# Ordering a product-key router's keys by summed exponentials instead of counts

## The chip, the cores and the metric

One core of one Trainium2 chip runs the kernel in one launch. Its engines, by the names of the profile, are PE (matrix products; PEld is its weight load), DVE (vector), ACT (scalar functions), POOL (which also issues the indirect gathers) and SP (which issues most plain transfers). Each works through an instruction list of its own, and they wait for each other on semaphores. The metric is device time of the launch in microseconds (us), lower is better.

## What the reference computes, where the change acts

The layer is an attention mixer on 512 tokens of 1024 features and then a product-key expert layer (PEER). Only the second is touched:

```python
q = (xb @ w_query).reshape(128, 8, 2, 128)               # 8 heads, two half queries
s = jnp.einsum('chpd,hpnd->chpn', q, sub_keys)           # scores against 128 keys per half
top_s, top_i = lax.top_k(s, 16)
cand_s = top_s[:, :, 0, :, None] + top_s[:, :, 1, None, :]
best_s, pos = lax.top_k(cand_s.reshape(128, 8, 256), 16) # 16 experts per token and head
g = jax.nn.softmax(best_s, axis=-1)
act = gelu(einsum('cd,chkd->chk', xb, expert_u[idx]))    # of 128 * 128 experts
out = einsum('chk,chkd->cd', g * act, expert_v[idx])
```

## The kernel before, in words

The experts of a head form a grid of 128 by 128 cells (key a of the first half, key b of the second). The kernel sorts both key lists of a head by popularity, and computes the 512 cells of a staircase in the popular corner (`RECTS`, rectangles of rows a0 to a1 and width w) densely for all 512 tokens, in four chunks of 128 experts per head. What a token chose outside the staircase is gathered: the tokens are sorted by how many such pairs they have, and each of the four sorted blocks of 128 tokens gets a fixed number of gathered columns (`TAIL`); what tokens have beyond goes to 128 further rows of `FOLD` = 4 pairs each. One column is one expert row (u and v, 8 KB) per token: a POOL gather of the expert's number (`tid`), a POOL gather of the row (`tuv`), a DVE product with the token's row that gives the dot product (`tscr`, L1903), and a DVE multiply-add to the token's sum (`tacc`, L1825). If 128 rows don't hold what is left, a loop (`tail_rest`) takes the remainder.

Time falls into three stages: the mixer (to about 350 us), the routing of the eight heads (to about 600 us), and the stage in which gathered columns are mixed with the rest of the dense experts (to about 1000 us), with a short end.

The routing runs in periods, one call of `route` per period i. A period mixes steps of four heads: L = head i (best 16 of both lists, pairs, best pairs), N = head i + 1 (second query, ranking of its keys, scores), M = head i + 2 (weights, first query), and B = head i - 1 (count, softmax weights, the dense cells' weights `dexp`). `dn(0)` to `dn(3)` put a quarter of a dense chunk each in between. Inside `in_order` every engine executes its instructions in the order in which the Python code emits them, so an instruction that waits holds back all that stands behind it on its engine. `best_pairs`, the last step of a period on DVE, yields the bound `tb` (L1357); ACT's count (`cm`, L1375) of the next period waits for it.

The ranking of N's keys (`rank1` to `rank3`, L1209 to L1255): PE computes the scores of the first block's 128 tokens (`pss`), DVE marks each token's best eight (`m8s`, `ind`), PE counts the marks of each key in two layouts (`psc`), DVE subtracts a tie-breaker (`pkey`), counts for each key how many keys are greater (`pjunk`, `prank`) and builds a permutation matrix (`pm`); `rank3` lets PE permute the keys (`psk`), ACT copies them (`kp`), and DVE forms the table of expert numbers (`tabs`, L1250), which SP stores.

Of the kernel before, what the change touches and what calls it, by code (L numbers as in the profile page):

```python
# [17 lines left out]
T = 512  # L18
D = 1024
NB = 4  # L20
# [10 lines left out]
# Cells (a, b) of a head's key grid, in popularity order, whose experts are computed for all tokens.  # L31
RECTS = ((0, 2, 60), (2, 6, 31), (6, 14, 20), (14, 32, 6))
CELLS = sum((a1 - a0) * w for a0, a1, w in RECTS)
NCH = CELLS // 128
# Gathered pairs per token, for the four blocks of tokens sorted by their number. What tokens have beyond goes to 128
# more rows of FOLD pairs each, as many to a token as it needs. When those don't do, a loop takes the rest instead.
TAIL = (29, 21, 16, 11)
# [18 lines left out]
# What the steps of dense and gathered experts take of the tensor engine, of the memory's bandwidth and of the vector  # L56
# engine, relative to each other.
# [9 lines left out]
# Ranks (a, b) of the two key lists that can be among the 16 best sums: (a + 1) * (b + 1) <= 16.  # L67
# [96 lines left out]
def build(tc, A, out):  # L164
    nc = tc.nc
    with ExitStack() as ctx:
# [9 lines left out]
        # The two parts of the rows that the large products take: the mixer's input, its outcome, the experts' input.  # L176
# [12 lines left out]
def rsq_steps(nc, y, t, v):  # L189
    """y = 1 / sqrt(v) to float32's accuracy."""  # L190
    nc.vector.tensor_scalar(t.bitcast(I32), v.bitcast(I32), 1, None, op0=OP.arith_shift_right)
    nc.vector.tensor_scalar(y.bitcast(I32), t.bitcast(I32), -1, 0x5F3759DF, op0=OP.mult, op1=OP.add)
    for _ in range(3):
        yield
        nc.vector.scalar_tensor_tensor(t, y, -0.5, y, op0=OP.mult, op1=OP.mult)
        nc.vector.tensor_tensor(t, t, v, op=OP.mult)
        yield
        nc.vector.scalar_tensor_tensor(y, t, 1.5, y, op0=OP.add, op1=OP.mult)


def rsq(nc, pool, v, n):
    """1 / sqrt(v) of a [128, n] tile."""
# [7 lines left out]
def rsq1(nc, pool, ss, n):  # L210
    """1 / sqrt(mean + EPS) of n values, from two sums of squares, in steps; h: minus half the mean."""
# [19 lines left out]
def sum_sq(nc, G, pool, ss, x, first, last, bufs=2):  # L231
    """Adds the squares of a tile [features, T] to the tokens' sums, [128, NB] of a bank."""
# [21 lines left out]
def row_bcast_of(nc, G, cols, pool, PS, tag, ptag=None):  # L254
    """Columns [128, n] as a row of 128 n tokens on all partitions; returns what does the product, to PSUM."""
# [18 lines left out]
def norm_shift(nc, hH, hL, z, sh):  # L274
    """The modulated rows in two parts."""
# [6 lines left out]
def load_split(tc, pool, src, tag, eng, raw=2, bufs=2, rpool=None):  # L282
    """A weight tile as float32r parts: high bits, and what they leave."""
# [7 lines left out]
def split(nc, pool, w, tag, eng, bufs=2):  # L291
    """High bits, and what they leave."""
# [16 lines left out]
def ada(tc, A, G, pool, m, ca, w):  # L309
    """Sums of a modulation's products over each partition's rows, in steps; loads run one ahead. For all but the first,  # L310
    scalar and GpSimd engines share the work, as the vector engine has other work then."""
# [31 lines left out]
def ada_start(tc, A, G, P1, AD, PS, m, ca, bcol):  # L343
    """A modulation whose products the tensor engine shares, as it has nothing else to do at the start; in steps."""
# [55 lines left out]
def ada_rest(tc, A, G, P1, PS, ca, bcol):  # L400
    """The modulations that the start doesn't need, in 43 steps."""
# [83 lines left out]
class Outward:  # L485
    """The outward projection by halves of the tokens: x1, and its rows for the experts."""
# [10 lines left out]
    def prepare(self, n):  # L497
        """The two parts of the weights' tiles up to n, one step per tile; loads run one ahead. They lie where the
        modulations' weights and the first head group's queries and keys were."""
# [36 lines left out]
    def after(self, half, i):  # L536
        """A tile's squares and its rows of tokens."""
# [21 lines left out]
    def finish(self, half):  # L559
        """A half's normed rows; in steps."""  # L560
# [23 lines left out]
def start(tc, A, G, P1, AD, PW, PS, S, xT, ca, bcol):  # L584
    """The first two modulations; the normed input, scaled, is in km."""
# [3 lines left out]
    # Rows of zeros: the scores' products span the whole array.  # L589
# [34 lines left out]
def project(tc, A, G, W, P1, PW, PS, S, lgain, band, rest, ahead):  # L624
    """The inward projections; what follows a tile's products comes after the next tile's."""
# [52 lines left out]
    def parts(dst, low, src, r):  # L678
        """High bits to some rows, and what they leave to others."""
# [3 lines left out]
    def rotate(i):  # L683
        """Rotary positions, and the parts that the scores' products take."""
# [84 lines left out]
def attention(tc, A, G, P1, PW, more, ups, PS, S, sink, nsink, band, mH, mL, rest, X, out):  # L769
    """Heads in three stages that run a few heads apart: scores, transposes, values. The first heads run beside the  # L770
    last of the projections (ups), whose memory is the attention's after that (more)."""
# [61 lines left out]
    def after(B):  # L833
        """What makes the normed rows of a block of tokens; in steps, the first of which follows the first group."""
# [87 lines left out]
def peer(tc, A, G, DR, out, xpool):  # L922
    nc = tc.nc
    with ExitStack() as ctx:
# [17 lines left out]
        with ExitStack() as c2:  # L942
            # The queries' weights lie where the attention was, so that they are there before the mixer's end.
# [18 lines left out]
            def step(amount):  # L962
                """Dense experts' steps where the routing leaves the tensor engine to them."""
# [26 lines left out]
def start_query(H):  # L990
    """The first head's queries, by halves of the tokens, and the second head's weights."""
# [14 lines left out]
def start_routing(tc, G, H):  # L1006
    """The first head's keys, and the experts' input as rows of tokens for the gathers."""
    nc = tc.nc
    with tc.tile_pool(name="h2p", bufs=1, side="right") as W:
# [9 lines left out]

        H[0].rank1()  # L1020
        rows(0)
        H[0].rank2()
        rows(1)
# [9 lines left out]
def end_routing(tc, A, G, B, WQ, step):  # L1033
    """The last head's weights, and the tokens' order."""
# [34 lines left out]
def first_columns(tc, G, WQ, step):  # L1069
    """The codes of the first gathered columns, and where their experts' rows are."""  # L1070
# [17 lines left out]
def in_order(tc):  # L1088
    """Keeps each engine's instructions in the order they are written in."""
# [1037 lines left out]
```

## Time and profile before

| | |
|---|---|
| median of 3 timed runs | 1040.32 us (1039.12 to 1043.28) |
| span of the profiled execution | 1042.5 us |
| PE, DVE, POOL, ACT busy over the span | 89%, 77%, 54%, 42% |
| mean granted TensorE clock | 0.955 of full speed |
| gathered columns | 81 |

The profiled execution is one of its own. Its span, from the first instruction to the last, is 1042.5 us, 2.2 us over the median of the timed runs and inside their range; what lies around a span is not listed, so the span is read as that execution's time.

### The profile page before, as it was taken

The page shows a single profiled execution, that of the slowest core. Times are in us where ns is not written, and L with a number is a line of the kernel's source. Part 1 is how long each engine was busy: PE and PEld are TensorE (multiplying, and loading weights), DVE is VectorE, ACT ScalarE, POOL GpSimd, SP SyncE. Part 2 cuts the span into 40 slices and gives each one's busy share as a digit, 9 for nine tenths or more (in the row PEclk, how much of TensorE's full clock was granted, in tenths as well). Part 3 has the DMA queues.
Part 4 walks back from the last instruction along what each step waited for, and adds up shares of the span by engine and source line. Part 5 has one row for each costly group of instructions (what it writes and reads, how often), then busy time and mean ns, then how long its engine had stood idle before and what let it go on. Part 6 is the DMA issues. An engine that isn't in the chain of part 4 may idle for free.

```text
span 1042.5 us, 13550 instructions
## 1 busy us (share of the span) xinstructions
PE 928.5 (89%) x4190; PEld 646.5 (62%) x4190; DVE 806.8 (77%) x2284; ACT 439.4 (42%) x937; POOL 565.7 (54%) x569
## 2 busy tenths in 40 slices
PE   7898989999999987898867889899999999999992
PEld 2475648788799776676654457365565747475640
DVE  4628756875555579999999768998668897887987
ACT  2334366555523436677765443042231414142312
POOL 1145711323432268777766375688657767577513
PEclk9999999996899999999988989999999999999997
DMA  8564132421221335453322476986959978788642
GB/s 325 205 229 163 61 114 83 168 86 58 85 76 41 134 115 163 123 156 109 105 68 78 126 292 248 343 324 211 325 212 370 395 255 319 293 326 284 231 168 83
DMA packets 77047, 196.86 MB, mean 189 GB/s; under 512 B 23271, under 2 KB 41063, under 8 KB 64871
## 3 DMA queue, kind: packets, MB, share of 16 engines
q0 software_dynamic: 26400, 118.93, 31.5%
q1 hardware_dynamic: 49848, 76.40, 21.8%
q8 instruction: 33, 0.54, 0.2%
q10 hardware_dynamic: 720, 0.62, 0.2%
q14 instruction: 46, 0.37, 0.1%
HBM read 187.95 MB, written 18.96 MB: 198 GB/s over the span
## 4 chain that ended last, share of the span: by engine, by line
PE 34%; DVE 34%; DMA 7%; issue 6%; POOL 3%; ACT 3%; SPq 0%; DVEq 0%; POOLq 0%; ACTq 0%
PE vacc L1604 9%; DMA tuv<-in_UV,tid 6%; PE udot L1553 5%; PE outp L305 4%; PE ops L831 4%; DVE dexp L1423 2%; DVE tacc L1825 2%; PE sc L807 2%; PE pt L815 2%; DVE tscr L1903 2%; PE q L1201 2%; DVE ti L1295 1%; DVE ti L1299 1%; DVE s L1293 1%; DVE cc L1327 1%
## 5 line engine op out<-in xcount | busy, mean ns | idle before, releaser
L1604 PE MATMUL vacc<-dv,gT 128*128 128x512 f32 x512 | 226.3, 599 | 5.4 <-DVE accd L1578 4.3
L1604 PEld LDWEIGHTS vacc<-dv,gT 128*128 128x128 f32 x512 | 97.7, 192 | 126.2 <-issue 112.5
L1903 DVE SCALAR_TENSOR_TENSOR tscr<-tuv,thp 128x1024 bf16<-128x1024 f32 x81 | 98.8, 1219 | 35.2 <-DMA tuv<-in_UV,tid 35.1
L1825 DVE SCALAR_TENSOR_TENSOR tacc<-tuv,twg,tacc 128x1024 f32<-128x1024 f32 x81 | 103.8, 1281 | 16.1 <-ACT twg L1824 15.9
L156 POOL DMA_INDIRECT tid<-tab,tci x81 | 94.6, 1168 | 29.4 <-issue 23.0
L1553 PE MATMUL udot<-hH,uh 128*128 128x512 f32 x256 | 108.5, 424 | 0.0
L156 POOL DMA_INDIRECT tuv<-in_UV,tid x81 | 93.6, 1155 | 27.0 <-issue 15.8
L1553 PE MATMUL udot<-hH,ul 128*128 128x512 f32 x256 | 102.8, 402 | 0.0
L1553 PE MATMUL udot<-hL,uh 128*128 128x512 f32 x256 | 102.4, 400 | 0.0
L1823 ACT ACTIVATE twg<-tdots 128x1 f32<-128x1 f32 x81 | 16.4, 202 | 149.1 <-DVE tscr L1903 149.1
L327 POOL TENSOR_TENSOR ada_acc<-ada_acc,ada_w 128x1024 f32<-128x1024 f32 x9 | 21.4, 2383 | 88.1 <-issue 30.7
L809 ACT ACTIVATE psb<-psb,anm 128x512 f32<-128x512 f32 (+2 forms) x64 | 40.9, 640 | 56.6 <-DVE psb L808 35.4
L297 POOL TENSOR_TENSOR wl_in<-wraw_in,wh_in 128x1024 fp32r<-128x1024 f32 x10 | 26.0, 2602 | 69.7 <-ACT wh_in L296 69.6
L1190 POOL TENSOR_TENSOR wl_pq<-wraw_pq,wh_pq 128x1024 fp32r<-128x1024 f32 x16 | 38.0, 2378 | 44.3 <-ACT wh_pq L1189 35.4
L1201 PE MATMUL q<-hH,wh_pq 128*128 128x512 f32 (+1 forms) x144 | 56.6, 395 | 0.1
L1553 PEld LDWEIGHTS udot<-hH,ul 128*128 128x128 f32 x256 | 49.0, 191 | 12.2 <-issue 0.2
L1201 PE MATMUL q<-hH,wl_pq 128*128 128x512 f32 (+1 forms) x144 | 54.9, 382 | 1.8 <-POOL wl_pq L1190 1.8
L1538 ACT CAST uh<-ut 128x512 fp32r<-128x512 f32 x64 | 37.3, 583 | 45.2 <-PE ut L1535 45.2
L1201 PE MATMUL q<-hL,wh_pq 128*128 128x512 f32 (+1 forms) x144 | 55.0, 383 | 0.5 <-DVE hL L580 0.5
L1553 PEld LDWEIGHTS udot<-hL,uh 128*128 128x128 f32 x256 | 49.3, 193 | 9.3 <-issue 0.2
L1553 PEld LDWEIGHTS udot<-hH,uh 128*128 128x128 f32 x256 | 49.2, 192 | 8.5 <-issue 0.2
L1546 ACT CAST ul<-ut 128x512 fp32r<-128x512 f32 x64 | 37.4, 584 | 36.0 <-PE ut L1545 35.7
(409 smaller groups left out, 2379.5 us busy)
## 6 DMA issues: line engine op xcount, KB each, us to landing
ada_w<-in_w_ada SPq DMA_DIRECT2D x22, 1024.0 KB
wraw_pq<-in_w_pq SPq DMA_DIRECT2D x16, 512.0 KB
gts<-gts SPq DMA_DIRECT2D x32, 256.0 KB
gT<-gts SPq DMA_DIRECT2D x32, 256.0 KB
wraw_in<-in_w_in SPq DMA_DIRECT2D x10, 512.0 KB
wraw_out<-in_w_out SPq DMA_DIRECT2D x8, 512.0 KB
x1T<-in_xT SPq DMA_DIRECT2D x4, 512.0 KB
ada_w<-in_w_ada SPq DMA_DIRECT2D x4, 512.0 KB
```

The costliest lines, as they stand in the source:

```text
L156: nc.gpsimd.indirect_dma_start(out=out, out_offset=None, in_=src, in_offset=bass.IndirectOffsetOnAxis(ap=idx, axis=0), **kw)
L305: nc.tensor.matmul(ps, a[:, c], b[:, c], start=n == 0, stop=n == 3 * kc - 1)
L809: nc.scalar.activation(U.p, U.p, AF.Exp, bias=nm, scale=-1.0, accum_out=B.den[:, i:i + 1])
L831: nc.tensor.matmul(B.ops[U.grp][:, U.h], U.pt[:, j], vr, start=j == 0, stop=j == U.nk - 1)
L1190: nc.gpsimd.tensor_tensor(wl, self.raw[p], wh.bitcast(F32), op=OP.subtract)
L1201: nc.tensor.matmul(self.q[p][:, cols], a[:, c], b[:, c, cols], start=c == 0 and i == 0, stop=c == KC - 1 and i == 2)
L1538: nc.scalar.copy(uh, pt)
L1546: nc.scalar.copy(ul, pt)
L1553: nc.tensor.matmul(ps, a, b[:, k], start=k == 0 and i == 0, stop=k == KC - 1 and i == 2)
L1604: nc.tensor.matmul(ps, ws[h, k][:, b * 128:(b + 1) * 128], vs[k][:, sl], start=k == 0, stop=k == NCH - 1)
L1825: nc.vector.scalar_tensor_tensor(acc, uv[:, D:], wg, acc, op0=OP.mult, op1=OP.add)
L1903: nc.vector.scalar_tensor_tensor(B.s, uv[:, 0:D], 1.0, B.hp, op0=OP.mult, op1=OP.mult, accum_out=B.dots[:, c])
```

## The change

The popularity of a key becomes the sum over all 512 tokens of exp(0.085 * score), where it was the number of the first 128 tokens that have the key among their best eight. `rank0(p)` computes a half's scores with the keys on partitions (one product of 128x512) and sums their exponentials with one ACT instruction. `rank1` turns the two sums into an ordering key (the upper bits of the number, minus the tie-breaker), copies it along a row on ACT (`pkeyb`) and lets PE transpose that to a row of all keys on every partition (`psc`). `rank2` compares as before. The staircase has five rectangles for four, still 512 cells. `TAIL` goes from 77 to 71 columns, 75 with the four of `FOLD` for 81. Comments are also dropped, which moves line numbers.

```diff
-RECTS = ((0, 2, 60), (2, 6, 31), (6, 14, 20), (14, 32, 6))
+RECTS = ((0, 2, 51), (2, 6, 28), (6, 14, 17), (14, 26, 8), (26, 48, 3))
+KEYSCALE = 0.085
+KEYBITS = 15
-TAIL = (29, 21, 16, 11)
+TAIL = (28, 20, 14, 9)
...
+    def rank0(self, p):
+        nc, R = self.nc, self.R
+        if p == 0:
+            self.stat = R.tile([128, 2], F32, name="stat", bufs=2)
+        ps = self.G.PS.tile([128, T], F32, name="pst", tag="rank")
+        nc.tensor.matmul(ps, self.keys[:, 0, p], self.q[p], start=True, stop=True)
+        junk = R.tile([128, T], BF16, name="pexp", bufs=1)
+        nc.scalar.activation(junk, ps, AF.Exp, scale=KEYSCALE, accum_out=self.stat[:, p:p + 1])
     def rank1(self):
-        for p in range(2):
-            nc.tensor.matmul(pss[:, p], self.q[p][:, 0:128], self.keys[:, 0, p], start=True, stop=True)
-        for p in range(2):
-            nc.vector.max(m8[:, p], pss[:, p])
-        for p in range(2):
-            nc.vector.tensor_scalar(self.ind[:, p], pss[:, p], m8[:, p, 7:8], None, op0=OP.is_ge)
+        bits = R.tile([128, 2], I32, name="pbits", bufs=1)
+        nc.vector.tensor_scalar(bits, self.stat.bitcast(I32), KEYBITS, None, op0=OP.arith_shift_right)
+        self.key = R.tile([128, 2], F32, name="pkey", bufs=2)
+        nc.vector.tensor_tensor(self.key, bits, G.noff, op=OP.subtract)
+        kb = R.tile([128, 2, 128], F32, name="pkeyb", bufs=1)
+        nc.scalar.copy(kb, self.key[:, :, None].to_broadcast([128, 2, 128]))
+        self.psc = G.PS.tile([128, 2, 128], F32, name="psc", tag="rank")
+        for p in range(2):
+            nc.tensor.transpose(self.psc[:, p], kb[:, p], G.ident)
     def rank2(self):
-        nc.tensor.matmul(psc[:, 0:256], G.onesb, self.ind.rearrange("p a b -> p (a b)"), start=True, stop=True)
-        for p in range(2):
-            nc.tensor.matmul(psc[:, 256 + p:257 + p], self.ind[:, p], G.onesb[:, 0:1], start=True, stop=True)
-        nc.vector.tensor_tensor(key, psc, G.noff, op=OP.subtract)
         for p in range(2):
-            nc.vector.tensor_scalar(junk, key[:, p * 128:(p + 1) * 128], key[:, 256 + p:257 + p], None,
-                                    op0=OP.is_gt, op1=OP.add, accum_out=rank[:, p:p + 1])
+            nc.vector.tensor_scalar(junk, self.psc[:, p], self.key[:, p:p + 1], None, op0=OP.is_gt, op1=OP.add,
+                                    accum_out=rank[:, p:p + 1])
...
 def route(G, H, dn, i):
     on(B, "count", 2)
+    on(N, "rank0", 0)
     on(N, "query", 1, 0, KC)
...
     dn(0)
     on(B, "weights")
-    on(N, "rank1")
+    on(N, "rank0", 1)
     for b in range(NB):
         on(B, "scale", b)
     if N is not None:
         G.gelu()
     on(L, "best", 1, 0)
+    on(N, "rank1")
     on(M, "query", 0, 0, 4)
```

On PE, in the fourth period, the list before has the ranking's two small products between the dense step (`udot`) and M's first query (`q`); the counts (`psc`) come twelve query products later.

```order
L1553 MATMUL udot<-hL,uh 128x512
L1553 MATMUL udot<-hH,ul 128x512
L1215 MATMUL pss<-keys,qsb 128x128 x2
L1201 MATMUL q<-hH,wh_pq 128x512
L1201 MATMUL q<-hL,wh_pq 128x512
```

With the change the second half's score product (`pst`) and, right behind it, the transposes of the copied key (`psc`) stand at that place, ahead of M's query.

```order
L1562 MATMUL udot<-hL,uh 128x512
L1562 MATMUL udot<-hH,ul 128x512
L1217 MATMUL pst<-qsb,keys 128x512
L1232 MATMUL psc<-ident,pkeyb 128x128 x2
L1203 MATMUL q<-hH,wh_pq 128x512
L1203 MATMUL q<-hL,wh_pq 128x512
```

So `psc` has moved from behind twelve query products to ahead of them, and reads `pkeyb`, which ACT writes.

On ACT, the same period before, from B's second count to the copy of the turned dense rows (`uh`): the copy of N's second query (`qsb`), B's exponentials and their scaling (`dexp`), and the dense step's gelu (`act`) with its table load.

```order
L1375 ACTIVATE cm,cn<-cand,tb 128x512 x2
L1205 COPY qsb<-q 128x512
L1416 ACTIVATE dexp<-cand,nmx 128x512 x4
L1546 CAST ul<-ut 128x512
L1419 ACTIVATE dexp<-dexp,rzk 128x512 x4
L1558 ACT_TABLE_LOAD
L1558 ACTIVATE act<-udot 128x512
L1538 CAST uh<-ut 128x512
```

With the change:

```order
L1382 ACTIVATE cm,cn<-cand,tb 128x512 x2
L1219 ACTIVATE pexp,stat<-pst 128x512
L1207 COPY qsb<-q 128x512
L1423 ACTIVATE dexp<-cand,nmx 128x512 x4
L1555 CAST ul<-ut 128x512
L1219 ACTIVATE pexp,stat<-pst 128x512
L1426 ACTIVATE dexp<-dexp,rzk 128x512 x4
L1567 ACT_TABLE_LOAD
L1567 ACTIVATE act<-udot 128x512
L1229 COPY pkeyb<-pkey 128x256
L1547 CAST uh<-ut 128x512
```

Two exponentials (`pexp`) have come in, and the copy `pkeyb` stands behind the scaling, the table load and the gelu. The number of table loads in the whole list stays the same.

## Rows read from the trace of the kernel before

**Rows 1.** Windows, one period: us, then busy us of each engine, clock, DMA share, GB/s.

```profile
core 0: us, PE busy (x) PEld busy (x) DVE busy (x) ACT busy (x) POOL busy (x), PEclk, DMA share, GB/s
444.10:472.40 28.30, 25.77 (x135) 20.65 (x134) 27.67 (x137) 20.19 (x35) 21.41 (x32) 1.00 0.57 166
```

**Rows 2.** Timeline of DVE, that period: start, duration, then the idle time and its releaser.

```profile
443.99 0.15 DVE L1357 TENSOR_TENSOR tb<-tb,mx 128x4 f32<-128x4 f32 x1
...
451.75 0.48 DVE L1217 MAX8 m8s<-pss 128x8 f32<-128x128 f32 x2
...
452.67 0.47 DVE L1291 MAX8 lb<-ssb 128x8 f32<-128x128 f32 x2
...
456.74 0.41 DVE L1228 TENSOR_TENSOR pkey<-psc,noff 128x258 f32<-128x258 f32 x1
457.19 0.35 DVE L1233 TENSOR_SCALAR_CACHE_REDUCE pjunk<-pkey 128x128 bf16<-128x128 f32 x1
...
461.50 0.35 DVE L1250 TENSOR_SCALAR tabs<-psk,c 128x128 int32<-128x128 f32 x1
...
472.24 0.17 DVE L1357 TENSOR_TENSOR tb<-tb,mx 128x4 f32<-128x4 f32 x1
```

**Rows 3.** Timeline of ACT, that period.

```profile
444.18 0.72 ACT L1375 ACTIVATE cm<-cand,tb 128x512 bf16<-128x512 f32 x1 [1.29 <-DVE tb L1357]
445.02 0.72 ACT L1375 ACTIVATE cm<-cand,tb 128x512 bf16<-128x512 f32 x1
...
451.93 2.56 ACT L1419 ACTIVATE dexp<-dexp,rzk 128x512 f32<-128x512 f32 x4 [0.18 <-DVE rzk L1396]
...
455.80 0.60 ACT L1558 ACTIVATE act<-udot 128x512 f32<-128x512 f32 x1
456.29 0.58 ACT L1538 CAST uh<-ut 128x512 fp32r<-128x512 f32 x1
...
459.70 0.37 ACT L1246 COPY kp<-psk 128x256 f32<-128x256 f32 x1 [2.34 <-PE psk L1244]
```

**Rows 4.** Timeline of PE, that period.

```profile
448.87 0.49 PE L1215 MATMUL pss<-keys,qsb 128*128 128x128 f32 x2 [0.61 <-ACT qsb L1205]
449.11 0.48 PE L1201 MATMUL q<-hH,wh_pq 128*128 128x512 f32 x1
...
458.28 0.95 PE L1242 MATMUL psk<-pm,keys 128*128 128x128 f32 x4 [0.27 <-DVE pm L1236]
...
459.20 0.47 PE L1244 MATMUL psk<-pm,prow 128*128 128x128 f32 x2
```

**Rows 5.** Chain that ended last, dense work in the gathering stage.

```profile
816.03 0.44 PE ut L1535 x4
816.46 1.40 PE udot L1553 x6
...
829.91 27.47 PE vacc L1604 x64
```

**Rows 6.** ACT and DVE timelines, the third period and the fifth.

```profile
425.29 2.56 ACT L1419 ACTIVATE dexp<-dexp,rzk 128x512 f32<-128x512 f32 x4 [0.19 <-DVE rzk L1396]
...
434.24 0.35 DVE L1250 TENSOR_SCALAR tabs<-psk,c 128x128 int32<-128x128 f32 x1
...
484.06 0.60 ACT L1558 ACTIVATE act<-udot 128x512 f32<-128x512 f32 x1
...
490.16 0.35 DVE L1250 TENSOR_SCALAR tabs<-psk,c 128x128 int32<-128x128 f32 x1
```

**Rows 7.** Windows around two waits of PE, columns as in Rows 1.

```profile
392.50:396.00 3.50, 0.21 (x2) 0.21 (x2) 3.43 (x23) 3.47 (x9) 3.17 (x3) 1.00 0.89 301
396.00:400.00 4.00, 4.00 (x13) 3.13 (x13) 3.65 (x14) 2.94 (x6) 3.36 (x8) 0.57 0.48 185
...
540.00:546.00 6.00, 4.41 (x20) 4.04 (x19) 5.86 (x16) 1.59 (x5) 5.69 (x8) 0.50 0.22 49
```

**Rows 8.** Windows of the gathering stage, columns as in Rows 1.

```profile
600.00:700.00 100.00, 87.75 (x320) 56.87 (x319) 86.62 (x205) 33.34 (x73) 69.69 (x65) 0.95 0.84 309
700.00:1000.00 300.00, 292.85 (x1034) 179.56 (x1033) 247.69 (x416) 88.69 (x235) 202.44 (x170) 1.00 0.79 287
```

**Rows 9.** The gathered rows' tile: operation, count, ns min/median/max, first and last start.

```profile
L1903 DVE SCALAR_TENSOR_TENSOR tscr<-tuv,thp x81: 1155/1218/1286, 618.2 to 996.7; 128x1024 bf16<-128x1024 f32 x81
L1825 DVE SCALAR_TENSOR_TENSOR tacc<-tuv,twg,tacc x81: 1271/1280/1347, 621.9 to 999.2; 128x1024 f32<-128x1024 f32 x81
```

**Rows 10.** DMA queue: packets, MB, share of 16 engines.

```profile
q0 software_dynamic: 26400, 118.93, 31.5%
```

More of the change, by code (lines that the diff above doesn't have):

```diff
@@ L1018, in rows @@
             nc.sync.dma_start(G.hs[b * 128:(b + 1) * 128, :], t)
+        H[0].rank0(0)
+        rows(0)
+        H[0].rank0(1)
+        rows(1)
         H[0].rank1()
-        rows(0)
         H[0].rank2()
-        rows(1)
         H[0].rank3()
@@ L1154, in route_setup @@
     nc = tc.nc
-    G.onesb = R.tile([128, 128], BF16, name="onesb")
-    nc.vector.memset(G.onesb, 1.0)
     G.irow = R.tile([128, 128], F32, name="irow")
@@ L1160, in route_setup @@
     iota(nc, G.prow, [[0, 128]], cm=1)
-    G.noff = R.tile([128, 258], F32, name="noff")
-    iota(nc, G.noff[:, 0:256].rearrange("p (a b) -> p a b", a=2), [[0, 2], [1, 128]])
-    iota(nc, G.noff[:, 256:258], [[0, 2]], cm=1)
+    G.noff = R.tile([128, 2], F32, name="noff")
+    iota(nc, G.noff, [[0, 2]], cm=1)
     nc.vector.tensor_scalar(G.noff, G.noff, 1.0 / 256, None, op0=OP.mult)
@@ L1206, in query @@
             self.q[p] = qt
-    def rank1(self):
-        nc, R = self.nc, self.R
-        pss = self.G.PS.tile([128, 2, 128], F32, name="pss", tag="rank")
-        m8 = R.tile([128, 2, 8], F32, name="m8s", bufs=2)
-        self.ind = R.tile([128, 2, 128], BF16, name="ind", bufs=1)
-        for p in range(2):
-            nc.tensor.matmul(pss[:, p], self.q[p][:, 0:128], self.keys[:, 0, p], start=True, stop=True)
-        for p in range(2):
-            nc.vector.max(m8[:, p], pss[:, p])
-        for p in range(2):
-            nc.vector.tensor_scalar(self.ind[:, p], pss[:, p], m8[:, p, 7:8], None, op0=OP.is_ge)
+    def rank0(self, p):
[6 more added lines that the diff above has]
+        nc.scalar.activation(junk, ps, AF.Exp, scale=KEYSCALE, accum_out=self.stat[:, p:p + 1])
+    def rank1(self):
+        nc, R, G = self.nc, self.R, self.G
+        bits = R.tile([128, 2], I32, name="pbits", bufs=1)
[5 more added lines that the diff above has]
+        self.psc = G.PS.tile([128, 2, 128], F32, name="psc", tag="rank")
+        for p in range(2):
+            nc.tensor.transpose(self.psc[:, p], kb[:, p], G.ident)
     def rank2(self):
         nc, R, G = self.nc, self.R, self.G
-        psc = G.PS.tile([128, 258], F32, name="psc", tag="rank")
-        nc.tensor.matmul(psc[:, 0:256], G.onesb, self.ind.rearrange("p a b -> p (a b)"), start=True, stop=True)
-        for p in range(2):
-            nc.tensor.matmul(psc[:, 256 + p:257 + p], self.ind[:, p], G.onesb[:, 0:1], start=True, stop=True)
-        key = R.tile([128, 258], F32, name="pkey", bufs=1)
-        nc.vector.tensor_tensor(key, psc, G.noff, op=OP.subtract)
         rank = R.tile([128, 2], F32, name="prank", bufs=2)
```

## The prediction, made before the changed kernel was run

> **What bounds the kernel now.** I read the windows by stage first, then, since they pointed at the routing, one of its periods on three engines, and last the gathering stage. A routing period is bound by DVE: of 28.3 us it is busy 27.67, PE 25.77, ACT 20.19 [rows 1]. The reader should see a loop in it. DVE ends a period with `tb` at 443.99; ACT's count starts at 444.18, released by it [rows 2, 3]; ACT then runs with hardly a wait until the gelu, whose successor starts at 456.29 [rows 3]. PE meanwhile serves the ranking: `psk` at 458.28 waited 0.27 us for DVE's `pm`, and its last record ends at 459.67 [rows 4]. ACT copies `kp` by 460.07 [rows 3], and DVE comes to `tabs` at 461.50 with all that ready, and to the next `tb` at 472.24 [rows 2]. So the products on PE have 1.4 us in hand before DVE needs them, and ACT has its own work done before PE asks for anything but `qsb`.
>
> The gathering stage is bound by PE: 87.75 busy of 100 us and then 292.85 of 300 [rows 8], and inside that the products follow each other without a gap: six of 512 columns in 1.40 us, which is 0.233 each, and 64 records of `vacc` in 27.47 us; these are 32 products of the program, 0.86 us each [rows 5]. DVE is at 247.69 of 300 there.
>
> **What the change does, part by part.**
>
> *DVE in the routing.* Gone are the marks (451.75 to 452.67, so 0.92 us) and the subtraction on 258 columns (456.74 to 457.19, 0.45) [rows 2]. New are two instructions on 128x2; the nearest row is `tb` on 128x4 at 0.15 [rows 2], and as the second waits for the first I take 0.4 for both. The comparisons stay. About 1.0 us per head is saved, 7 us over the seven periods that rank a head, if DVE stays the bound.
>
> *PE in the routing.* New are two products with 512 columns in full precision, 0.86 each [rows 5], and two transposes, half of the 0.44 us of four [rows 5]; gone is about half a microsecond of `pss` (its successor starts 0.24 us after its second pair) and of `psc`. That makes some 1.4 us more per period, against 2.5 us in which PE was not busy [rows 1]. By itself it would hide.
>
> *ACT in the routing.* New are two exponentials of 128x512 with a sum. The nearest rows are the counts, same shape and also summed, 0.84 us apart [rows 3]: 1.68. The copy `pkeyb` is like `kp`, 128x256, 0.37 [rows 3]. ACT has 8 us of slack per period, but these land where it has none.
>
> *The wait that the change adds.* PE's transposes `psc` need `pkeyb`. On ACT that copy stands behind count, exponentials, scaling, table load and gelu; on PE everything of the period from M's query on stands behind `psc`. Walk the fourth period. The gelu's successor started at 456.29; the two exponentials push that by 1.68, of which 0.18 falls into the wait for `rzk` before the scaling [rows 3], so `pkeyb` starts at 457.8 and ends at 458.2. `psc` ends at 458.4. Now PE does what it had begun at 449.11 [rows 4]: twelve query products (12 x 0.233 = 2.8), the dense quarter (0.44 + 1.40), four turns of `dexp` (0.44), six query products (1.40) [rows 5], and `psk`, which took from 458.28 to 459.67 (1.39) [rows 4]. That is 7.9 us, so `psk` ends at 466.3, where it ended at 459.67. Then `kp` (0.37) and 0.2 for the instruction ahead of `tabs`: 466.8, against 461.50 [rows 2]. DVE waits there with `tabs`, and its whole remainder to `tb`, which starts the next period's ACT work, comes 5.3 us later. DVE's saved microsecond is inside that wait and buys nothing.
>
> The same walk for the third period, which has no gelu yet: the scaling starts at 425.29 and takes 2.5, plus 1.68 less the 0.19 waited, so `pkeyb` ends at 429.6 and `tabs` comes at 438.3 against 434.24 [rows 6]: +4.0. For the fifth, from the gelu at 484.06, whose successor comes 0.49 later as in the fourth [rows 3]: `pkeyb` ends at 486.4, `tabs` at 495.1 against 490.16 [rows 6]: +4.9. The sixth repeats the fifth: +4.9. In the second the dense step is smaller; its price lies between nothing and the third's, and I take 2. In the seventh no M is left, so nothing stands between `psc` and `psk`: 1, with 0 and 2 as bounds. At the start and in the first period no B loads ACT, so `psc` waits only for exponential, DVE's two instructions and copy (0.84 + 0.4 + 0.37), but PE is what the stage runs on; with the new products I take 4 for both together, with 0 and 6 as bounds. Sum: 4 + 2 + 4.0 + 5.3 + 4.9 + 4.9 + 1 = 26 us.
>
> *The clock.* In those periods PE would sit still from the end of `pst` to `psc`, 5 to 8 us. [...] 0.43 of 4 us at half speed is a loss of 1.7 us, on the stretch from `psc` to `psk` that ends the loop. Five periods: 8.5 us. The bounds are 0 and, if the clock stays at half as it did from 540 to 546 with PE busy three quarters [rows 7], the whole 7.9 us again per period, 39. I take 8.5, since after `psc` PE has work without a gap, as in the window at 0.57.
>
> *Fewer columns.* Six of 81 go: on DVE 6 x (1.22 + 1.28) = 15 us [rows 9], on POOL twelve gathers, about 6 MB of transfers. The stage lasts as long as PE's dense work, and PE stood idle 12.2 and 7.2 us in it [rows 8]; that 19 us is all that fewer columns can give back. Columns are spread over the dense steps by share, so the last one ends at the same dense step as before. I take 4 us, with 0 and 12 as bounds.
>
> *The rest.* A fifth rectangle means two more POOL additions for the cells and two small ones for the pairs per head, and one more store on SP; POOL is busy 21.4 of 28.3 us [rows 1], a cover of 7 us, and longer periods widen it.
>
> Together 26 + 8.5 - 4 = +30 us. The profiled execution, 1042.5 us, would become 1073; it lies 2.2 us over the median of the runs, so I predict **1071 us**.
>
> **The rivals.**
>
> *Absorbed, and faster.* If `pkeyb` came by 452.9, 5.3 us before my walk has it, or if the query products could pass the waiting transposes, `tabs` would not be late, DVE would stay the bound, and the result would be 1040.3 - 7 - 4 = 1029. For it speaks DVE's load in the period [rows 1]. Against it: when the second half's `pss` waited 0.61 us for `qsb`, the query product behind it started only at 449.11, after it [rows 4]. [...]
>
> *The columns set the gathering stage.* 81 columns take from 618.2 to 999.2, 4.7 us each [rows 9]; six would be 28 us, and the result 1071 + 4 - 28 = 1047, or 1039 without the loss of clock. Against it stands the gapless PE [rows 5, 8]. [...]
>
> *The clock stays low.* At half speed from `psc` to `psk` in five periods: 31 us more, about 1101.
>
> *The staircase doesn't hold enough.* Then the loop for the rest runs, 32 columns at no less than 4.7 us: over 1190. Routing the reference's inputs by both rules gives 9026 gathered pairs before and 8291 after, and 111 and 109 of the 128 further rows. The count of before fits the profile: 9026 rows of 8 KB are 73.9 MB, the dense rows 33.6, the blocks' rows and residuals 11, together 118.5 of 118.93 MB [rows 10]. So the columns fit, if closely.
>
> **How the numbers follow.** Chances: the opened loop as forecast 0.73, with 1056 to 1086 as its own range; absorbed 0.08; columns set the stage 0.07; clock stays low 0.08; loop for the rest 0.04. No change from no change can be told within 0.5%, 1035.1 to 1045.5. Faster: the absorbed case, 0.08. Within: the better part of the columns' case, 0.05. Slower: 0.87. The range 1044 to 1094 holds nearly all of the first case, half of the columns' and half of the clock's.
>
> **What would show it.** In the changed trace: PE idle 5 to 8 us before `psc` in periods two to six, released by ACT's `pkeyb`; a granted clock well under 1 just behind; DVE idle before the instructions of `rank2` and `rank3`, released by PE or by `kp`; `tb` to `tb` 32 to 36 us in the fourth period, where it was 28.3; the gathering stage as long as before within a few us, with 75 columns. The prediction is wrong if `tb` to `tb` stays under 29 us, if the wait before `psc` is short, or if the gathering stage shortens by over 12 us.

## The result, and the profile after

The changed kernel takes 1068.82 us (median of four runs, 1067.14 to 1069.21) and the kernel before 1040.98 (median of four, 1039.12 to 1043.28). The ratio on record is 1.0258, with a 95% interval of 1.0224 to 1.0293; the quotient of the two medians is 1.0267. Ratios here and below leave out executions that took over 1.5% longer than the fastest of the same kernel. The profiled execution has a span of 1067.0 us, 24.5 over that of before. PE is busy 88%, DVE 73%, POOL 53%, ACT 42% of it, and the mean granted clock is 0.946. The execution took 1068.83 us; so a span is not the whole time of its execution, as was assumed ahead of the prediction, but 1.8 us less. The forecast comes to the median plus its sum all the same, so this doesn't touch it.

The difference is read from one start of `tb` to the next, in the seven routing periods from the second to the eighth. Before they take 26.43, 26.64, 28.25, 27.68, 27.70, 25.55 and 23.92 us, together 186.2; with the change 30.34, 30.86, 34.13, 32.50, 33.18, 26.76 and 23.93, together 211.7. That is +25.5. From the last `tb` to the end it was 465.4 us and is 466.8.

The rows that answer to [rows 1] and [rows 7] are windows of the changed kernel's fourth period, 449.71 to 483.84, and of three pieces in it:

```profile
core 0: us, PE busy (x) PEld busy (x) DVE busy (x) ACT busy (x) POOL busy (x), PEclk, DMA share, GB/s
449.70:483.80 34.10, 27.75 (x131) 22.27 (x130) 24.26 (x133) 20.89 (x39) 21.78 (x37) 0.85 0.51 141
464.00:468.00 4.00, 3.91 (x11) 3.14 (x12) 3.15 (x8) 0.04 (x1) 3.69 (x7) 0.50 0.50 153
468.00:472.00 4.00, 4.00 (x18) 3.19 (x17) 1.03 (x3) 0.59 (x1) 3.65 (x7) 0.73 0.15 30
472.00:476.00 4.00, 4.00 (x27) 3.56 (x26) 0.79 (x4) 1.84 (x4) 0.00 (x0) 1.00 0.21 68
```

DVE, which bound this period before, now idles 9.8 of 34.1 us, and no other engine is busy throughout in its place. In the list of waits between 390 and 560 us (total us, times, longest) the longest of PE and of DVE are these two, and behind them one more of DVE:

```profile
PE psc L1232 <- ACT pkeyb L1229: 29.3, 5, 6.5
DVE c L1255 <- ACT kp L1253: 26.6, 5, 6.1
...
DVE pjunk L1240 <- PE psc L1232: 6.0, 3, 3.1
```

The timelines of the fourth period, for [rows 2 to 4]: first ACT, from the count to the copies.

```profile
450.09 0.72 ACT L1382 ACTIVATE cm<-cand,tb 128x512 bf16<-128x512 f32 x1 [0.95 <-DVE tb L1364]
...
454.16 0.58 ACT L1219 ACTIVATE pexp<-pst 128x512 bf16<-128x512 f32 x1
...
461.86 1.28 ACT L1567 ACT_TABLE_LOAD   x1
463.15 0.60 ACT L1567 ACTIVATE act<-udot 128x512 f32<-128x512 f32 x1
463.64 0.40 ACT L1229 COPY pkeyb<-pkey 128x256 f32<-128x256 f32 x1
474.68 0.37 ACT L1253 COPY kp<-psk 128x256 f32<-128x256 f32 x1 [1.69 <-PE psk L1251]
```

Then PE, the transposes of the key, the first product behind them, and the end of `psk`:

```profile
464.09 0.69 PE L1232 MATMUL psc<-ident,pkeyb 128*128 128x128 f32 x2 [6.35 <-ACT pkeyb L1229]
464.43 0.78 PE L1203 MATMUL q<-hH,wh_pq 128*128 128x512 f32 x1
...
474.18 0.47 PE L1251 MATMUL psk<-pm,prow 128*128 128x128 f32 x2
```

And DVE:

```profile
449.71 0.34 DVE L1364 TENSOR_TENSOR tb<-tb,mx 128x4 f32<-128x4 f32 x1
...
460.22 0.16 DVE L1227 TENSOR_TENSOR pkey<-pbits,noff 128x2 f32<-128x2 int32 x1
464.82 0.35 DVE L1240 TENSOR_SCALAR_CACHE_REDUCE pjunk<-psc,pkey 128x128 bf16<-128x128 f32 x1 [3.11 <-PE psc L1232]
...
475.09 0.16 DVE L1255 TENSOR_SCALAR c<-psk 128x1 f32<-128x1 f32 x1 [6.02 <-ACT kp L1253]
475.36 0.35 DVE L1257 TENSOR_SCALAR tabs<-psk,c 128x128 int32<-128x128 f32 x1
...
483.84 0.34 DVE L1364 TENSOR_TENSOR tb<-tb,mx 128x4 f32<-128x4 f32 x1
```

One chain runs through the three lists. DVE has the key at 460.38, and ACT comes to copy it at 463.64. PE has stood still for 6.35 us when the copy is there and takes up M's query at half speed (granted clock 0.50), and DVE stands still for 6.02 us until the permuted keys come back.

In the gathering stage the windows are those of [rows 8], 23 us later as the last `tb` is, and the tile's row answers to [rows 9]:

```profile
623.00:723.00 100.00, 87.22 (x320) 55.92 (x319) 85.48 (x207) 33.01 (x71) 65.88 (x63) 0.97 0.81 296
723.00:1023.00 300.00, 294.15 (x1030) 180.70 (x1029) 232.07 (x391) 86.05 (x225) 192.69 (x160) 0.98 0.76 271
```

```profile
L1912 DVE SCALAR_TENSOR_TENSOR tscr<-tuv,thp x75: 1162/1218/1227, 643.8 to 1021.2; 128x1024 bf16<-128x1024 f32 x75
```

DVE has lost 15.6 of its 247.69 us there, PE nothing. `tscr` comes 75 times, and its last start lies 377.4 us behind its first, where it was 378.5 with 81.

### The profile page after: what moved, and what is told of

Same layout as the page of the kernel before. It is cut to its first block, busy times and chain, and to the rows that moved or that the text cites. A ratio compares the mean times of both kernels' runs of the same rounds, so it can differ in the third digit from the quotient of the medians.

```text
span 1067.0 us, 13520 instructions
## 1 busy us (share of the span) xinstructions
PE 937.4 (88%) x4182; PEld 647.9 (61%) x4182; DVE 781.5 (73%) x2230; ACT 448.2 (42%) x965; POOL 561.5 (53%) x588
## 3 DMA queue, kind: packets, MB, share of 16 engines
q0 software_dynamic: 25344, 112.90, 29.7%
## 4 chain that ended last, share of the span: by engine, by line
PE 49%; DVE 23%; ACT 7%; DMA 4%; issue 3%; POOL 2%; SPq 0%; DVEq 0%; POOLq 0%; ACTq 0%
PE vacc L1613 15%; PE udot L1562 11%; PE q L1203 4%; PE outp L308 4%; PE ops L834 3%; PE ut L1544 2%; PE sc L810 2%; PE pt L818 2%; DVE tscr L1912 2%; DVE tacc L1834 1%; DMA tuv<-in_UV,tid 1%; PE foldp L1960 1%; DMA gts<-gts 1%; PE ut L1554 1%; ACT dexp L1426 1%
## 5 line engine op out<-in xcount | busy, mean ns | idle before, releaser
L1912 DVE SCALAR_TENSOR_TENSOR tscr<-tuv,thp 128x1024 bf16<-128x1024 f32 x75 | 91.3, 1218 | 28.6 <-DMA tuv<-in_UV,tid 28.5
L1834 DVE SCALAR_TENSOR_TENSOR tacc<-tuv,twg,tacc 128x1024 f32<-128x1024 f32 x75 | 96.2, 1282 | 21.2 <-ACT twg L1833 21.1
L159 POOL DMA_INDIRECT tuv<-in_UV,tid x75 | 90.8, 1210 | 23.2 <-issue 15.2
L159 POOL DMA_INDIRECT tid<-tab,tci x75 | 87.0, 1160 | 28.5 <-issue 19.9
L300 POOL TENSOR_TENSOR wl_in<-wraw_in,wh_in 128x1024 fp32r<-128x1024 f32 x10 | 25.5, 2546 | 70.6 <-ACT wh_in L299 70.6
L1203 PE MATMUL q<-hH,wh_pq 128*128 128x512 f32 (+1 forms) x144 | 62.4, 435 | 0.0
L1203 PE MATMUL q<-hL,wh_pq 128*128 128x512 f32 (+1 forms) x144 | 57.4, 400 | 0.5 <-DVE hL L583 0.5
L1203 PE MATMUL q<-hH,wl_pq 128*128 128x512 f32 (+1 forms) x144 | 57.3, 399 | 0.4 <-POOL wl_pq L1192 0.4
L159 POOL DMA_INDIRECT dv<-in_UV,cid x32 | 36.8, 1151 | 38.5 <-PE vacc L1613 31.1
L1555 ACT CAST ul<-ut 128x512 fp32r<-128x512 f32 x64 | 37.5, 585 | 40.4 <-PE ut L1554 40.4
```

Of the source, the lines that this page charges most:

```text
L159: nc.gpsimd.indirect_dma_start(out=out, out_offset=None, in_=src, in_offset=bass.IndirectOffsetOnAxis(ap=idx, axis=0), **kw)
L1203: nc.tensor.matmul(self.q[p][:, cols], a[:, c], b[:, c, cols], start=c == 0 and i == 0, stop=c == KC - 1 and i == 2)
L1555: nc.scalar.copy(ul, pt)
L1834: nc.vector.scalar_tensor_tensor(acc, uv[:, D:], wg, acc, op0=OP.mult, op1=OP.add)
L1912: nc.vector.scalar_tensor_tensor(B.s, uv[:, 0:D], 1.0, B.hp, op0=OP.mult, op1=OP.mult, accum_out=B.dots[:, c])
```

## The experiments

On the chips of these runs the kernel before took 1055.9 to 1063.0 us (medians), against 1041.0 above. Behind the routing, the traces from them show single pauses of 2 to 10 us on PE, ACT and DVE for which no releaser is seen, and from the last `tb` to the end 481 to 504 us with 75 or 81 columns. Expectations below that name 455 to 471 us for that stretch, or a whole time in us, are not met there, for this reason; the kernel before has 503.0 there itself in its second profile. So whole times are compared as ratios to the kernel before on the same chip, and mechanisms by the seven routing periods: the kernel before gave 186.2 and 186.7, the changed kernel 211.7 twice.

**Theory.** The loop was opened at `psc`: the late copy holds PE's whole list, the loss of clock adds to it, and the columns are worth little. **Rivals.** The new work itself (two score products, two transposes, two exponentials) costs the time; or the columns pace the gathering stage.

**1. PE's transposes behind M's query.** `rank1` was split, and the transposes became a step of their own:

```diff
...
     on(N, "rank1")
     on(M, "query", 0, 0, 4)
+    on(N, "rank1t")
     on(B, "dense2", 0)
...
```

> The changed kernel with one move: PE's two transposes of the copied key stand behind M's first twelve query products, not ahead of them. Theory (all of a period on PE is held back behind the transposes): the products, 5.1 us at the half clock in the fourth period, come off the stretch from the transposes to psk, so each of periods two to six is 3 to 5 us shorter, the first about 1.5, and the whole is 1069 - 15 to 25 = 1044 to 1054 us, with PE's wait before the transposes down from 6.4 to 1 to 4 us. Rival (the cost is ACT's longer list, whatever PE does meanwhile): 1064 to 1069 us, periods as in the changed kernel.

Measured 1.0107 (1.0048 to 1.0167); the seven periods sum to 197.0, 14.7 less than with the change. PE's waits for the key copy between 385 and 560 us fall from 29.3 to 19.0 us:

```profile
PE psc L1237 <- ACT pkeyb L1230: 19.0, 6, 6.3
```

I repeated it beside other kernels:

> Again the changed kernel with the transposes of the key behind the first query's twelve products on PE, all else as in the change, beside the others on one chip. Theory: the seven periods sum to 197 us as in the first look, first tb near 389, the last tb to the end 467, so 1050 to 1056. Rival (the order on PE is worth nothing in the whole, because the later stage takes it back): 1065 or more.

Measured 1.0106 (1.0011 to 1.0200), periods 191.4. Twelve products at another place in one list give back 15 to 20 of 25.5 us, with every new instruction still there: most of the cost is the place, not the work. The clock has a part in it, and in the difference between the two: behind the transposes of the sixth period it was 0.50 for 4 us in the first profile and 1.00 in the second, and from them to the end of `psk` it took 7.56 and 4.98 us. In absolute time this chip's 1064 says nothing, since before took 1055.9 there.

**2. The copy on DVE.** The same place in the program, another engine:

```diff
-        nc.scalar.copy(kb, self.key[:, :, None].to_broadcast([128, 2, 128]))
+        nc.vector.tensor_copy(kb, self.key[:, :, None].to_broadcast([128, 2, 128]))
```

> The changed kernel with one move: the key is copied along its row by DVE right behind its own two small instructions, not by ACT behind scaling, table load and gelu. Theory (the copy's place in ACT's list sets when PE goes on): the copy ends at 460.7 where it ended at 464.0 in the fourth period, and so in the fifth to seventh; in the second and third ACT's copy already waited for the key, and nothing is won. 3.3 us in three or four periods: 1069 - 10 to 13 = 1056 to 1059 us. Rival (PE's own new products and the lower clock are the cost): 1066 to 1070 us.

Measured 1.0216 (1.0097 to 1.0335), periods 203.9. PE's timeline of the fourth period:

```profile
460.88 0.66 PE L1232 MATMUL psc<-ident,pkeyb 128*128 128x128 f32 x2 [3.09 <-DVE pkeyb L1229]
```

The wait is half as long, and 7.8 us of the periods come back, where 10 to 13 were expected. The whole is 1.0216 of before, some 1063 us on the first chip's scale, between the theory's range and the rival's; with that interval the whole does not tell them apart, and only the periods speak for the theory. What remains of the wait is that DVE itself reaches the key late, behind the third best-16 step (`best(1, 0)`).

**3. Work for PE in the wait.** Twenty products that nobody reads, into M's query bank, ahead of the transposes:

```diff
...
     on(N, "rank1")
+    if i >= 1:
+        on(M, "fill", 20)
+    on(N, "rank1t")
     on(M, "query", 0, 0, 4)
...
```

> The changed kernel with 20 more products of 512 columns ahead of the transposes in periods two to six, into the bank that M's query overwrites afterwards: 4.7 us of work that PE does while it would wait. Nothing is left out. Theory for the clock term: the granted clock behind the transposes is 0.9 or more, where it was 0.50 to 0.64 over 4 us, and each of five periods is 1.5 to 3 us shorter: 1069 - 8 to 14 = 1055 to 1061 us. Rival (the lower clock falls where it costs nothing, only the wait counts): 1067 to 1070 us. If the added products lie on the path in periods with short waits, up to 1072.

Measured 1.0193 (1.0098 to 1.0289), periods 202.6. The fourth went from 34.13 to 31.38. PE's timeline there, and the windows behind it:

```profile
454.16 5.21 PE L1216 MATMUL q<-hH,wh_pq 128*128 128x512 f32 x20
461.08 0.44 PE L1243 MATMUL psc<-ident,pkeyb 128*128 128x128 f32 x2 [1.72 <-ACT pkeyb L1236]
...
468.41 0.47 PE L1262 MATMUL psk<-pm,prow 128*128 128x128 f32 x2
```

```profile
461.00:465.00 4.00, 3.92 (x20) 3.29 (x21) 3.41 (x9) 0.24 (x2) 3.77 (x6) 1.00 0.48 151
465.00:469.00 4.00, 4.00 (x26) 3.46 (x26) 0.40 (x2) 1.05 (x3) 3.69 (x8) 1.00 0.32 85
```

The key is no earlier relative to the loop (`pkeyb` starts 13.94 us behind `tb`, 13.93 with the change), PE does more work, and 9.1 us come back. The granted clock stays at 1.00 where it was 0.50 and then 0.73, and from the transposes to the end of `psk` it takes 7.80 us where it took 10.56: all that the period has won. Over the five periods this stretch takes 37.5 us for 48.6, at a clock of 1.00 throughout; 2 of these 11.1 us don't come back, since in the second and third period PE, with the added products ahead, comes to the transposes 1.1 and 0.7 us later behind `tb` than with the change. That is the clock's term of the sum, measured by itself.

**4. The old staircase and 81 columns.** `RECTS` and `TAIL` of the kernel before, everything else changed.

> The changed kernel with the staircase and the columns of the kernel before: four rectangles and 81 columns, the new ordering kept. Theory (PE's dense work sets the gathering stage, and columns lie beside it): 0 to 4 us longer, 1068 to 1073 us, the stage from the last tb to the end as long as with 75 columns within 3 us. Rival (columns pace the stage, 4.7 us each): 1069 + 28 = 1097 us.

Measured 1.0299 (1.0202 to 1.0395), periods 211.0. Repeated:

> Again the changed kernel with the staircase of four rectangles and the 81 columns of before, beside the others on one chip. Theory (six columns fewer are worth 0 to 4 us): 1067 to 1073, the last tb to the end 466 to 471. Rival (4.7 us a column): 28 us more, 1097.

Measured 1.0223 (1.0127 to 1.0319), periods 211.3. The changed kernel has 1.0258 and, below, 1.0209. Within these intervals the worth of the six columns can't be told from nothing; 28 us, or 2.7%, would have shown.

**5. Sixty columns.** The second edit switches off the loop for the rest, so the pairs that don't fit are left out.

```diff
-TAIL = (28, 20, 14, 9)
+TAIL = (22, 16, 11, 7)
...
-    nc.vector.tensor_scalar(G.nit, G.nit, 3, None, op0=OP.arith_shift_right)
+    nc.vector.tensor_scalar(G.nit, G.nit, 16, None, op0=OP.arith_shift_right)
```

> The changed kernel with 60 gathered columns for 75 (TAIL 22, 16, 11, 7 and the four of FOLD) and the loop for the rest switched off, so that the pairs that do not fit are left out. Theory (PE's dense work sets the gathering stage): from the last tb to the end it takes 455 to 467 us (466.8 in the changed kernel), and the whole is 1055 to 1069. Rival (the columns pace the stage at 4.7 us each): 70 us less, about 998. In between, 2 us a column, would be 1039.

Measured 1.0487 (1.0359 to 1.0616). The stage from the last `tb` took 500.3 us. Neither my theory nor the rival had that, so I repeated it beside the unchanged kernels:

> The changed kernel with 60 gathered columns again, loop for the rest off and the pairs that do not fit left out, beside the kernel with 75. Theory (PE's dense steps set the stage, whatever the columns): the dense steps come 6.9 us apart and the changes of chunk 34.4 apart as with 75 columns, and the whole lies within 10 us of the changed kernel. Rival one (the columns pace it): 4.7 us less for each of 15 columns, ratio to before 0.96. Rival two (the first look: fewer columns make the stage longer): 20 us or more over the changed kernel on the same chip.

> The changed kernel, unchanged, beside the kernel before on one chip. Theory (the change's cost lies in the routing alone): routing periods 211 to 212 us, 25 more than before's, start 0 to 5 more, and from the last tb to the end the same as the kernel before within the scatter of that stage; ratio about 1.026. Rival (the stage behind it is also longer with the change): over 5 us more there in the middle of several runs, ratio 1.03 or more.

> The kernel before, unchanged, profiled beside the other three of this group on one chip, to read each stage's length there. Theory: seven routing periods 186 us whatever the chip; from the last tb to the end 465 us or longer, and whatever it is longer by comes from pauses of the engines that the profile shows no releaser for, with products at a lower granted clock behind them.

Before gave 1060.27 us against 1060.06 of itself; the changed kernel 1082.93, ratio 1.0209 (1.0154 to 1.0263); sixty columns 1108.07, ratio 1.0412 (1.0348 to 1.0477). For the changed kernel that speaks for its theory (about 1.026) over its rival (1.03 or more). For sixty columns rival two holds: fewer columns made this kernel 25 us longer than the changed one. The routing is not in it (211.7 us in both), and the dense steps are not either. In the changed kernel's first profile their gelus come in this rhythm:

```profile
719.43 0.60 ACT L1567 ACTIVATE act<-udot 128x512 f32<-128x512 f32 x1 [0.81 <-PE udot L1562]
726.37 0.60 ACT L1567 ACTIVATE act<-udot 128x512 f32<-128x512 f32 x1 [0.80 <-PE udot L1562]
733.33 0.60 ACT L1567 ACTIVATE act<-udot 128x512 f32<-128x512 f32 x1 [0.81 <-PE udot L1562]
779.58 0.60 ACT L1567 ACTIVATE act<-udot 128x512 f32<-128x512 f32 x1 [0.81 <-PE udot L1562]
```

6.9 us within a chunk; at a change of chunk 34.4 at the least, here 46.2, since the sum of the further rows (`foldp`) waits in PE's list there. With 60 columns the steps still come 6.9 apart and not closer, but for the last of all, which is 5.6 in every run. What differs is where a block's end stands among them. The last change of chunk there, on PE (up to 1075 us) and on DVE:

```profile
1042.34 1.88 PE L1613 MATMUL vacc<-dv,gT 128*128 128x512 f32 x4
1051.20 2.08 PE L1613 MATMUL vacc<-dv,gT 128*128 128x512 f32 x2 [6.99 <-DVE gT L1575]
1056.53 18.95 PE L1613 MATMUL vacc<-dv,gT 128*128 128x512 f32 x38 [3.25 <-DMA dv<-in_UV,cid]
```

```profile
1044.36 1.23 DVE L2036 TENSOR_TENSOR tacc<-tacc,gf 128x1024 f32<-128x1024 f32 x1
1049.32 1.22 DVE L2037 TENSOR_TENSOR tx<-tx,tacc 128x1024 f32<-128x1024 f32 x1 [3.73 <-DMA tx<-x1s,perm]
1050.46 1.28 DVE L1575 TENSOR_TENSOR gT<-act,gT 128x512 f32<-128x512 f32 x2
```

And the same place in the changed kernel beside it, PE and DVE:

```profile
1039.28 27.63 PE L1613 MATMUL vacc<-dv,gT 128*128 128x512 f32 x64
1040.11 0.69 DVE L1575 TENSOR_TENSOR gT<-act,gT 128x512 f32<-128x512 f32 x1 [0.43 <-ACT act L1567]
...
1045.82 1.23 DVE L2037 TENSOR_TENSOR tx<-tx,tacc 128x1024 f32<-128x1024 f32 x1
```

The columns ran out early, so the last block's end (`tx`) came to stand ahead of `gT` in DVE's list and waits for a transfer. PE waits for `gT`, then for the next `dv`, and goes on at half speed (a granted clock of 0.50 from 1051 to 1060 us). From the last gelu to the end this takes 65.5 us, against 47.0 in the changed kernel beside it (1108.0 less 1042.5, and 1086.5 less 1039.5); the remaining 3 us of the two spans' 21.5 lie earlier. The first profile with 60 columns has the same two waits of PE (6.96 and 3.43 us) and 65.6 us. So the number of columns acts here, as far as these traces show, through the order it produces, not through their work; no run changed that order by itself.

PE's weight loads are busy 180.70 of 300 us in the changed kernel's window above, its products 294.15. Judged by the loads alone, PE would have room; the run with a fifth fewer columns, whose dense steps still come 6.9 us apart, decides against that here.

**6. A ranking that holds nobody up.** DVE makes key and copy ahead of `best(1, 0)`, the transposes stand behind M's query, and the second half's score product goes between the turns of `dexp`. The edit of the copy is that of experiment 2, and `rank1` is split as in experiment 1.

```diff
...
-    for b in range(NB):
+    for b in range(2):
         on(B, "dense1", b)
     dn(0)
     on(B, "weights")
     on(N, "rank0", 1)
+    for b in range(2, NB):
+        on(B, "dense1", b)
...
-    on(L, "best", 1, 0)
     on(N, "rank1")
+    on(L, "best", 1, 0)
     on(M, "query", 0, 0, 4)
+    on(N, "rank1t")
...
```

> The changed kernel's ranking rearranged so that nothing is queued behind a late key: DVE makes the copy of the key, and does it with its two instructions ahead of the last best-16 step; PE's transposes stand behind the first query's twelve products; the second half's score product stands behind the first half of the four turns of dexp. Columns as in the change (75). Theory (the loop ACT copy, transposes, query, permutation was opened, and DVE's load is less than before): DVE is the bound of the routing again, the seven periods sum to 180 to 188 us (changed kernel 211.7, before 186.2), and the whole comes to 1036 to 1046. Rival one (the two new score products and two transposes on PE are what costs): the periods stay above 195, 1050 or more. Rival two (the clock is the cost): nothing of the sum returns except where PE's waits go, and the granted clock behind psc is still near half.

Measured 1.0102 (1.0013 to 1.0191), periods 188.0. The periods are as the theory had them, the whole is not, so it was run again with before and after beside it:

> The rearranged ranking again, beside before and after on one chip. Theory (the routing alone decides): routing periods 188 us as in the first look, so 0.995 to 1.005 of the kernel before. Rival (the 10 us by which it was longer than before in the first comparison are a part of the change that this does not undo, in the stage behind): 1.01, and that stage some 10 us longer than in the kernel before beside it.

Measured 0.9956 (0.9911 to 1.0001), periods 187.5. The medians of all its twelve executions and of the 23 of the kernel before, 1061.49 and 1060.06, give 1.0013. In the first profile the fourth period's transposes on PE start with no wait:

```profile
448.50 0.38 PE L1237 MATMUL psc<-ident,pkeyb 128*128 128x128 f32 x2
...
452.79 0.71 PE L1254 MATMUL psk<-pm,keys 128*128 128x128 f32 x4
```

With the new ranking in this order the seven periods are as long as before within 2 us (188.0 and 187.5 against 186.2 and 186.7); the start, from DVE's last `hL` to the first `tb`, is still 3.1 us longer (43.2 against 40.1). The periods aren't shorter, although DVE has lost the marks: the fourth is (26.6 against 28.25), the fifth is longer (30.05 and 29.34 against 27.68). The traces answer in part why the fifth is. In it the cast `fi` on DVE meets POOL's weight residual (last section) and takes 2.04 and 1.31 us, where the sixth has 0.20, and in the second profile DVE also waits 0.62 us for ACT's `pexp`. The first comparison puts the whole 0.1 to 1.9% over the kernel before, the second between 0.9% under and level. No version here beats the kernel before for certain.

## Why the prediction was right, point by point

The forecast was 1071 us by the opened loop; it took 1068.82 by the opened loop. The mechanism was right. That the number came so close is in part luck: two terms were off by 5 us each, with opposite signs, so that the rows of the change add up to 31.4 us in the two profiles (25.5 + 4.5 + 1.4) where 30.5 were forecast. A third difference has nothing to do with the change.

**The walk held, the remainder didn't.** From `tb` to `tabs` the third to the sixth period are later by 5.8, 8.1, 6.1 and 6.8 us (before by [rows 2, 6] and two more of the same row), 26.8 in all; the walk had 19.1 and with its clock 25.9. In the fourth, `pkeyb` starts 13.9 us behind `tb`, forecast 13.8. The step that failed was that "its whole remainder to `tb`" only moves: from `tabs` to `tb` it took 9.75, 10.74, 9.76 and 9.78 us before and takes 8.15, 8.48, 8.48 and 8.49, which is 6.4 given back (last section). So the periods two to eight cost 25.5 us where walk and clock had 30.6.

**The clock** was sized nearly rightly: 8.5 forecast; the fill gave back 9.1, and 11.1 on the stretch from `psc` to `psk` itself. The single periods differ more from the 1.7 taken for each: 1.4, 1.8, 2.8, 1.2 and 2.0 came back. In the fourth the clock was 0.50 and then about 0.73 for 4 us each, in the fifth 0.65 for 4 us and then 1.00; the forecast had 0.57 for 4 us, from the window behind 3.50 us in which PE was busy 0.21 [rows 7], and its 0.43 is what that window lacks of the full clock.

**Start and first period**: 44.53 us from DVE's last `hL` to the first `tb`, 40.05 before, in the two pairs of profiles alike. 4 was forecast, 4.5 it is.

**Fewer columns** was mis-sized: 4 us were taken, and the stage is 1.4 longer in the one pair of profiles from this chip; experiment 4 can't tell the six columns from nothing. The bounds had no loss in them, though a block's end must stand somewhere in DVE's list, and PE waits for what stands behind it. With 60 columns PE waited 6.99 us for `gT`, and the end of the kernel was 18.5 us longer in experiment 5 with such an order.

**What the two profiled executions differ in besides**: the mixer ended 6.9 us earlier in that of the changed kernel, where the window from 230 to 260 us had a clock of 0.94 against 0.66 in that of before. A second profile of the kernel before had 1.00 there, so this belongs to executions, not to kernels. 25.5 + 4.5 + 1.4 - 6.9 makes the 24.5 between the spans.

**The rivals.** Absorbed: no; `pkeyb` was not early, and no query product passed the waiting transposes. The product behind `psc` began 0.34 us after it, whose wait was 6.35. Columns pace the stage: no, by experiments 4 and 5. The clock stays low: no, it was back at 1.00 from 472 us on. The staircase held: no pass of the loop for the rest, 75 gathers of rows. Their queue moved 112.90 MB, 6.03 less than before [rows 10], which is the forecast difference of 9026 and 8291 rows of 8 KB (8192 bytes).

## What to carry to other kernels

Before a step is moved or given to another engine, write down for each in-order list what stands behind its waiting instruction; here two transposes, put ahead of twelve products that needed nothing from them, cost 15 to 20 us. A part of that is clock, which by itself, with the order left and the pause filled, was worth 9; the two overlap and don't add up. A new instruction belongs on the engine that has its input first and behind whatever its waiting engine could do meanwhile: of the periods' 25.5 us the copy on DVE gave back 7.8, the transposes behind M's query 14.7 and 20.3. Where work was taken here from an engine that doesn't set the stage, what was left, as far as the traces show, was the effect of the order that this changed: six columns fewer gave nothing that could be measured, and 15 fewer again made the kernel 25 us longer.

## What the runs showed of the hardware that was not expected

Some DVE instructions, sums of two inputs above all, took longer where they met an instruction of POOL. The same seven small sums (`cc`), in the fourth period before and then with the change, each with POOL's weight residual:

```profile
465.30 3.27 DVE L1327 TENSOR_TENSOR cc<-la,lb 128x64 f32<-128x64 f32 x7
465.30 2.46 POOL L1190 TENSOR_TENSOR wl_pq<-wraw_pq,wh_pq 128x1024 fp32r<-128x1024 f32 x1
...
470.38 0.35 DVE L1343 TENSOR_TENSOR gt<-cc,mx 128x200 f32<-128x200 f32 x1
```

```profile
478.34 0.77 DVE L1334 TENSOR_TENSOR cc<-la,lb 128x64 f32<-128x64 f32 x7
479.25 2.70 POOL L1192 TENSOR_TENSOR wl_pq<-wraw_pq,wh_pq 128x1024 fp32r<-128x1024 f32 x1 [7.37 <-ACT wh_pq L1191]
480.80 1.38 DVE L1350 TENSOR_TENSOR gt<-cc,mx 128x200 f32<-128x200 f32 x1
```

With POOL idle, in its wait for ACT, the sums took 0.77 us. Begun with the POOL instruction they took 3.27, of which one of the seven took 2.37, and ended 0.81 us behind it (468.57 and 467.76), as if that one had waited for its end. With the change POOL came later, after that wait of 7.37 us, and a DVE instruction further on, `gt`, met it instead and took 1.38 us, where it took 0.35 before. These two (-2.5 and +1.0) and two smaller ones (-0.8) make the 2.3 us which the fourth period's remainder gave back. It is plainest in the fifth period, where before a sum of 128x4 met the residual and ended with it (494.99 and 494.97), and with the change met nothing:

```profile
492.60 2.37 POOL L1190 TENSOR_TENSOR wl_pq<-wraw_pq,wh_pq 128x1024 fp32r<-128x1024 f32 x1 [0.42 <-ACT wh_pq L1189]
492.77 2.22 DVE L1409 TENSOR_TENSOR ns<-ns,nd 128x4 f32<-128x4 f32 x1
```

```profile
510.47 0.15 DVE L1416 TENSOR_TENSOR ns<-ns,nd 128x4 f32<-128x4 f32 x1
```

In the third and the sixth period it is `cc` (3.33 us for 0.77) and `ns` (2.22 for 0.14) in the same way, and `gt` meets the residual in all four with the change (1.38 to 1.53 us for 0.35). No run here took the POOL instruction away, so what makes the two meet in this way was not shown. The prediction did not weigh that a change of rhythm shifts such meetings.

The other surprise is the size of pauses without a releaser on other chips, as here on PE in a profile of the kernel before:

```profile
824.58 0.80 PE L1545 MATMUL ut<-uh,nident 128*128 128x512 f32 x1 [8.69 <-issue]
```

From the last `tb` to the end this execution took 503.0 us where the first profile of the same kernel took 465.4 and shows no such pause of over 2 us on PE in that stretch. It took 1079.4 us in all, where the median of its thirteen is 1060.27; but shorter executions on these chips show such pauses too, as one of 1057.83 us with the transposes behind M's query does, of 5.28 us on PE. The mean granted clock was 0.943 in that execution and 0.955 in the first profile. How much of the difference is the pauses and how much the lower clock was not separated, and what makes the pauses stays open.
